# adaLN weight pieces moved from SP's DMA queue to GpSimd's, one burst per projection unit from a single buffer

## The chip, the cores and the metric

The kernel runs on one core of a Trainium2 chip. Its time is the device time of one execution in microseconds (us), from the runs listed below; a further execution was recorded by the hardware profiler, and every duration below is from that trace. The engines have these names: PE is TensorE (PEld its weight loads), DVE is VectorE, ACT is ScalarE, POOL is GpSimd, SP is SyncE, which here only issues DMAs. SPq and POOLq are the issuing sides of SP and GpSimd.

## What is computed

One layer of a conditioned decoder, for a prompt of 256 tokens and for 8 sample sequences of 8 tokens (320 rows in all, width 2048), with weights shared by both. All arrays are float32.

```python
mod = silu(c) @ w_ada + b_ada                    # (9, 6*2048): one row per sequence
sh1, sc1, g1, sh2, sc2, g2 = split(mod, 6)
h = rmsnorm(x, norm1_g) * (1 + sc1) + sh1
q, k, v, og, u, ga, gb, alr = split(h @ w_in)
o, s_new = gla(q, k, v, log_sigmoid(alr @ w_a2 + b_a) / 16, state_gla)
y_a = rmsnorm(o, gla_norm_g) * silu(og)
y_b = pool(u) * pool_scale
x = x + g1 * ((sigmoid(ga) * y_a + sigmoid(gb) * y_b) @ w_o)
h2 = rmsnorm(x, norm2_g) * (1 + sc2) + sh2
gate, up = split(h2 @ w_gu, 2)
y = rmsnorm(x + g2 * ((silu(gate) * up) @ w_down), final_norm_g)
```

The "adaLN" part is the first line: w_ada has 6 sections of 2048 columns, 100 MB in all, multiplied by only nine rows. Sections 0 and 1 (sh1, sc1) are needed before the first projection, section 2 (g1) after w_o, sections 3 and 4 (sh2, sc2) before the FFN, and section 5 (g2) after w_down.

## The kernel before

**Projections.** Each weight matrix streams from HBM once. `raw_chunk` (L131) loads a piece of 4 k-tiles by 256 columns, 512 KB, through SP's queue into one of three raw buffers. `split` (L141) makes a high half (ACT, L146) and the low remainder (DVE, L147), in four buffers each of two k-tiles. `mm3` (L159 to L162) adds three matmuls per k-tile and 128 columns. A unit (`proj`, L164) is 256 columns by 16 k-tiles: 4 pieces, 2 MB, 96 matmuls. PE works through the units in order; SP issues a piece when the DVE has freed its raw buffer.

**Stages.** The head of the program normalizes x, computes sections 0 and 1 and projects head 0 of four; then come the other three heads, eleven units each (L902 to L922: q, k, two of v, u, two each of og, ga and gb). While a head's units run, the GLA and pooling steps of the head before are taken from a queue (`pump`, ten steps after each unit) and run between them. Then come w_o (eight units, L964), the second norm, and the FFN in two parts: w_gu, then w_down (L1010 on).

**adaLN bursts.** Sections 4, 2, 3 and 5 are made in "bursts" (L239, L240): 24 bursts of 256 columns by 16 k-tiles (2 MB, sections 4, 2, 3), then two of 512 columns by 16 k-tiles (4 MB) and four of 512 columns by 8 k-tiles (2 MB) for section 5. `ada_load` (L256) takes a buffer of 16 KB per partition (for the 4 MB bursts 32 KB), with the tag "big", and lists its pieces of 1 MB; `ada_piece` (L247) issues one of them on SP, after the last weight piece; `ada_burst` (L263) does its matmuls (L279, the activations stationary, w_ada moving), transposes the result back (L292) and adds it up (L294). In heads 1 to 3 there is a burst after each of the units 3 to 10, with two buffers and one burst ahead. Burst 25 and 26 are loaded during w_o, in pieces that `x1_and_ada` (L955) issues between weight pieces, and done after the second norm's sum (L987). The last four are loaded and done in the first part of the FFN.

**GLA states.** Per head the old states of 8 sequences are 4 MB. `s_load` (L731) loads half of the sequences, 2 MB as two DMAs (d = 0, 1) on GpSimd, into a buffer of the same tag "big" as the bursts. `s_inter` (L740) multiplies by them on PE (L747), `s_state` (L763) updates them on DVE (L770) and GpSimd stores them back (L772). A tile framework decides the order on each engine when the program is built, and puts in the waits for buffers and data.

Of the kernel before, what the change touches and what calls it, by code (L numbers as in the profile page):

```python
# [1 line left out]

# [1 line left out]

# [7 lines left out]
F32 = mybir.dt.float32  # L12
# [67 lines left out]
def body(tc, A):  # L80
# [13 lines left out]
    def nm(s):  # L94
        uid[0] += 1
        return "%s_%d" % (s, uid[0])
# [30 lines left out]

    more = []
    last_raw = []

    def raw_chunk(src, nk, nn, pool=None, tag="raw", bufs=3):  # L131

# [26 lines left out]
    def mm3(ps, whi, wlo, xhi, xlo, start, stop):  # L159
        PE.matmul(ps, lhsT=whi, rhs=xhi, start=start, stop=False)  # L160
        PE.matmul(ps, lhsT=whi, rhs=xlo, start=False, stop=False)  # L161
        PE.matmul(ps, lhsT=wlo, rhs=xhi, start=False, stop=stop)  # L162

    def proj(w, col, k0, k1, xh, xl, between=None):  # L164

# [78 lines left out]
    ada_want = []  # L244
    ada_ps = []

    def ada_piece():  # L247

        n, t, r = ada_want.pop(0)
        sec, b, nb, k0, nk = BURSTS[n]  # L250
        step = min(nk, 16 // nb)
        col = (sec * KT + b) * P
        with tc.issue_after(last_raw[0]):
            nc.sync.dma_start(t[:, r:r + step], wada[:, k0 + r:k0 + r + step, col:col + nb * P])

    def ada_load(n, bufs):  # L256

# [2 lines left out]
            t = ada_raw[n] = apool[0].tile([P, nk, nb * P], F32, tag="big", bufs=bufs, name=nm("araw"))  # L260
            ada_want.extend((n, t, r) for r in range(0, nk, min(nk, 16 // nb)))

    def ada_burst(ahead, bufs):  # L263

        n = len(ada_done)
        sec, b, nb, k0, nk = BURSTS[n]
        ada_done.append(n)
        ada_load(n, bufs)
        while ada_want and ada_want[0][0] <= n:
            ada_piece()  # L270
        w = nb * P
        if k0 == 0:
            ada_ps[:] = [misc()]
        ps = ada_ps[0]
        first = True
        with tc.high_priority():
            for r in range(nk - 4, -1, -4):
                for j in range(4):
                    PE.matmul(ps[32 * j:32 * j + 32, 0:w], lhsT=scT[:, k0 + r + j, :], rhs=ada_raw[n][:, r + j, :],  # L279
                              start=k0 == 0 and first, stop=k0 + nk == KT and r == 0, tile_position=(0, 32 * j))  # L280
                first = False
        for m in range(n + 1, n + 1 + ahead):
            ada_load(m, bufs)
# [26 lines left out]
    def s3(ap):  # L310
        return ap.rearrange("p (b t) -> p b t", t=LS)
# [229 lines left out]
    def gla_steps(g):  # L541
# [188 lines left out]

        def s_load(gg):  # L731
            def f():
                t = apool[0].tile([P, 2, 4, DV], F32, tag="big", bufs=2, name=nm("S0"))
                for d in range(2):
                    nc.gpsimd.dma_start(t[:, d], A["state_gla"][0, 4 * gg:4 * gg + 4, h, d * P:(d + 1) * P, :]
                                        .rearrange("b p e -> p b e"))
                    E["S0", gg, d] = t[:, d]
            return f

        def s_inter(gg):  # L740
# [158 lines left out]
                gates(g0, kind, i, getattr(g0, kind)[:, 2 * i:2 * i + 2, :])  # L899
    queue += pst + st[:PSY] + [sig0] + psy + st[PSY:] + [merge_step(g0, E)]  # L900
    RATE = 10
    for h in range(1, H):  # L902
        pump(RATE)
        g = new_group(h)
        for ui, (kind, i, col) in enumerate(units(h)):
            if kind == "og" and i == 0:
                pump(len(queue))
                new_gates(g)
            ps = proj(win, col, 0, KT, hh, hl)
            evac(ps, g, kind, i, None)  # L910
            if kind == "u":
                pump(len(queue))
                st, E = gla_steps(g)
                pst, psy = pool_steps(g)
                queue += pst + st
            if ui > 2:
                ada_burst(0 if ui == 10 else 1, 2)
                while ada_want:
                    ada_piece()
            pump(RATE)  # L920
        queue += psy + [merge_step(g, E)]
    pump(len(queue))  # L922
# [29 lines left out]

    xs = fp.tile([P, KT, TS], F32, name="xs")
    tiny = fp.tile([P, 1], F32, name="tiny")
    def x1_and_ada(c):  # L955

        if c == 0:
            with tc.issue_after(last_raw[0]):
                for k in (2 * ui, 2 * ui + 1):
                    nc.sync.dma_start(x1[k], xspill[k])  # L960
        elif c < 12 and ada_want:
            ada_piece()

    for ui in range(8):  # L964
        if ui == 0:
            ada_load(AMIX, 2)
            ada_load(AMIX + 1, 2)
        ps = proj(wo, 256 * ui, 0, KT, mh, ml, between=x1_and_ada)
        for i in range(2):
            residual(ps, i, 2 * ui + i, 2)  # L970
            k = 2 * ui + i
            sq_acc(acc, k, k == 0)
            G.tensor_tensor(s3(xs[:, k]), s3(x1[k][:, TP:T]), mods(4, k), op=ALU.mult)
        if ui == 6:
            S.activation(tiny, epst, AF.Sqrt)

# [7 lines left out]

    more[:] = [fa, None]
    rs = rstd_bcast(acc)
    ada_burst(0, 2)  # L987
    ada_burst(0, 2)
# [21 lines left out]
    for pi, (f0, f1) in enumerate(parts):  # L1010
        ah, al = {}, {}
        for f in range(f0, f1, 2):
            sg = fa.tile([P, 2, T], F32, tag="sg", name=nm("sg"))
            if f == 0:
                pg, pu = projs(((wgu, f * P), (wgu, FF + f * P)), 0, KT, h2h, h2l)
                S.activation(sg, pg[:, :, 0:T], AF.Silu)
            else:
                pg = proj(wgu, f * P, 0, KT, h2h, h2l)
                S.activation(sg, pg[:, :, 0:T], AF.Silu)
                pu = proj(wgu, FF + f * P, 0, KT, h2h, h2l)  # L1020
            V.tensor_tensor(sg, pu[:, :, 0:T], sg, op=ALU.mult)
            th = f2.tile([P, 2, T], F32R, tag="ah%d" % ((f - f0) // 2), name=nm("ah"))
            tl = f2.tile([P, 2, T], F32R, tag="al%d" % ((f - f0) // 2), name=nm("al"))
            hilo(th, tl, sg)
            for j in range(2):
                ah[f + j], al[f + j] = th[:, j], tl[:, j]
            if pi == 0 and f >= 2:
                if f == 2:
                    ada_load(AEND, 1)
                if f in (4, 8, 12, 16):  # L1030
                    ada_burst(1, 1)
                if ada_want:
                    ada_piece()
        if pi == 0:
            bcx.close()
        else:
            hcx.close()
            yp = ctx.enter_context(tc.tile_pool(name="yp", bufs=1, side="right"))
            yn = [yp.tile([P, D], F32, name="yn%d" % i) for i in range(3)]
            xgs = [yp.tile([P, 3 * P], F32, name="xg%d" % i) for i in range(2)]  # L1040
            for xg in xgs:
                G.memset(xg[:, T:3 * P], 0.0)
        for ui in range(8):
            ps = proj(wdn, 256 * ui, f0, f1, ah, al)
            for i in range(2):
# [12 lines left out]
            if pi == 1 and ui == 5:  # L1058
                S.activation(tiny, acc2[:, 0:1], AF.Sqrt)
# [44 lines left out]
```

## Time and profile before

| | |
|---|---|
| runs | 2012.51, 2013.57, 2014.87 us; median 2013.57 |
| the profiled execution | 2015.12 us, its span 2013.2 us |
| mean granted clock of PE | 0.991 |
| moved by DMA | 400.60 MB, mean 199 GB/s |
| weight pieces (w_in), issue to landing | 4.7 us median, 512 KB |
| adaLN pieces, issue to landing | 11.0 us median, 1 MB |
| GLA state loads, issue to landing | 8.7 us median, 1 MB |

The page is read like this. Its first part gives the busy time of each engine. The second cuts the span into 40 slices of some 50 us; a digit is the busy share in tenths, PEclk the clock that PE was granted, DMA the busy share of the 16 DMA engines. Further views give busy times by stretch, who waited for whom, the chain of waits that ended last, the instructions in order of time, and the DMA queues: q1 is the hardware queue that SP feeds, q0 the software queue that GpSimd feeds. A DMA row "on SPq" is the time in which the queue took the request, not the transfer. The head lies at 0 to 225 us, heads 1 to 3 at about 225 to 890, w_o to 1040, the FFN to 2000.

### The profile page before, as it was taken

How to read it: one execution, taken by the hardware profiler on the slowest of the kernel's cores; microseconds unless marked ns; L12 is line 12 of the kernel's file. 1: busy time of each engine (PE TensorE's matmuls, PEld its weight loads, DVE VectorE, ACT ScalarE, POOL GpSimd, SP SyncE). 2: the span in 40 equal slices, each digit the busy share in tenths (PEclk: the TensorE clock that was granted, in tenths of full speed). 3: DMA queues.
4: the chain of work that ended last, by engine and by line, in shares of the span. 5: the costliest groups of instructions: out<-in, count | busy, mean ns of one | idle time of the engine just before them, and what ended most of it. 6: DMA issues, size and time to landing. Idle time of an engine off the chain costs nothing.

```text
span 2013.2 us, 34658 instructions
## 1 busy us (share of the span) xinstructions
PE 1946.5 (97%) x13808; PEld 1824.4 (91%) x13808; DVE 1000.4 (50%) x1918; ACT 828.1 (41%) x1484; POOL 121.1 (6%) x228
## 2 busy tenths in 40 slices
PE   5999999999999999998999999999999999999997
PEld 3779998888998898987979999999999999999997
DVE  2655655555355535663565444444444444444554
ACT  3323634643344333552445333333333343344443
POOL 1002100210011001100021000000000000000000
PEclk9999999999999999999999999999999999999998
DMA  9996457559765987489735655444444444444443
GB/s 320 346 333 232 128 178 249 184 189 333 234 216 191 294 248 240 150 281 340 243 117 166 203 166 188 160 152 150 142 157 152 147 149 155 148 147 147 147 141 100
DMA packets 350236, 400.60 MB, mean 199 GB/s; under 512 B 12417, under 2 KB 322209, under 8 KB 349737
## 3 DMA queue, kind: packets, MB, share of 16 engines
q1 hardware_dynamic: 338122, 358.29, 56.8%
q0 software_dynamic: 11952, 40.10, 5.5%
q8 instruction: 108, 1.77, 0.4%
q14 instruction: 54, 0.44, 0.1%
HBM read 373.90 MB, written 24.67 MB: 198 GB/s over the span
## 4 chain that ended last, share of the span: by engine, by line
PE 83%; DMA 9%; DVE 3%; issue 2%; ACT 1%; SPq 1%; POOL 0%; ACTq 0%; DVEq 0%
PE ps L160 25%; PE ps L162 25%; PE ps L161 25%; DMA raw<-w_in 3%; DMA raw<-w_o 2%; PE pm L279 2%; PE pm L220 1%; DMA S<-state_gla 1%; PE pm L125 1%; DVE wlo L147 1%; DVE S L770 1%; DMA o_gs<-S 1%; PE pm L747 1%; DMA vr<-b_ada 1%; DMA araw<-w_ada 1%
## 5 line engine op out<-in xcount | busy, mean ns | idle before, releaser
L147 DVE TENSOR_TENSOR wlo<-raw,whi 128x512 fp32r<-128x512 f32 x952 | 655.3, 694 | 798.5 <-ACT whi L146 795.1
L146 ACT CAST whi<-raw 128x512 fp32r<-128x512 f32 x952 | 585.2, 622 | 917.4 <-PE ps L161 775.7
L160 PE MATMUL ps<-hh,whi 128*128 128x320 f32 x1408 | 444.2, 316 | 10.1 <-ACT whi L146 9.8
L162 PE MATMUL ps<-hh,wlo 128*128 128x320 f32 x1408 | 438.3, 313 | 1.9 <-DVE wlo L147 1.8
L161 PE MATMUL ps<-hl,whi 128*128 128x320 f32 x1408 | 439.6, 312 | 0.0
L160 PE MATMUL ps<-h2h,whi 128*128 128x320 f32 x1408 | 435.8, 310 | 0.0
L161 PE MATMUL ps<-h2l,whi 128*128 128x320 f32 x1408 | 435.6, 309 | 0.0
L162 PE MATMUL ps<-h2h,wlo 128*128 128x320 f32 x1408 | 435.3, 309 | 0.0
L160 PEld LDWEIGHTS ps<-hh,whi 128*128 128x128 f32 x1408 | 265.5, 189 | 34.2 <-ACT whi L146 14.3
L162 PEld LDWEIGHTS ps<-hh,wlo 128*128 128x128 f32 x1408 | 264.8, 189 | 13.8 <-DVE wlo L147 6.1
L161 PEld LDWEIGHTS ps<-hl,whi 128*128 128x128 f32 x1408 | 265.7, 189 | 7.6 <-issue 6.4
L161 PEld LDWEIGHTS ps<-h2l,whi 128*128 128x128 f32 x1408 | 264.3, 188 | 3.4 <-issue 3.4
L160 PEld LDWEIGHTS ps<-h2h,whi 128*128 128x128 f32 x1408 | 264.3, 188 | 0.8 <-ACT h2h L997 0.8
L162 PEld LDWEIGHTS ps<-h2h,wlo 128*128 128x128 f32 x1408 | 264.3, 188 | 0.0
L160 PE MATMUL ps<-ah,whi 128*128 128x320 f32 x704 | 217.7, 309 | 0.0
L161 PE MATMUL ps<-al,whi 128*128 128x320 f32 x704 | 216.5, 308 | 0.0
L162 PE MATMUL ps<-ah,wlo 128*128 128x320 f32 x704 | 216.5, 308 | 0.0
L161 PEld LDWEIGHTS ps<-al,whi 128*128 128x128 f32 x704 | 132.0, 187 | 0.0
L160 PEld LDWEIGHTS ps<-ah,whi 128*128 128x128 f32 x704 | 131.9, 187 | 0.0
L162 PEld LDWEIGHTS ps<-ah,wlo 128*128 128x128 f32 x704 | 131.9, 187 | 0.0
L160 PE MATMUL ps<-mh,whi 128*128 128x320 f32 x256 | 80.3, 314 | 9.7 <-ACT whi L146 9.7
L162 PE MATMUL ps<-mh,wlo 128*128 128x320 f32 x256 | 80.1, 313 | 0.2 <-DVE wlo L147 0.2
(279 smaller groups left out, 1532.8 us busy)
## 6 DMA issues: line engine op xcount, KB each, us to landing
raw<-w_gu SPq DMA_DIRECT2D x176, 512.0 KB, 3.6
raw<-w_in SPq DMA_DIRECT2D x173, 512.0 KB, 4.7
araw<-w_ada SPq DMA_DIRECT2D x64, 1024.0 KB, 11.0
raw<-w_down SPq DMA_DIRECT2D x80, 512.0 KB, 3.5
raw<-w_ada SPq DMA_DIRECT2D x64, 512.0 KB, 6.7
S<-state_gla POOLq DMA_DIRECT2D x16, 1024.0 KB, 8.7
o_gs<-S POOLq DMA_DIRECT2D x16, 1024.0 KB, 6.2
raw<-w_o SPq DMA_DIRECT2D x32, 512.0 KB, 5.9
```

The source lines that it names most:

```text
L125: PE.transpose(out, in_, ident[:k, :k])
L146: S.copy(hi, raw)
L147: V.tensor_sub(lo, raw, hi.bitcast(F32))
L160: PE.matmul(ps, lhsT=whi, rhs=xhi, start=start, stop=False)
L161: PE.matmul(ps, lhsT=whi, rhs=xlo, start=False, stop=False)
L162: PE.matmul(ps, lhsT=wlo, rhs=xhi, start=False, stop=stop)
L220: PE.matmul(ps[32 * j:32 * j + 32, 0:w], lhsT=scT[:, k0 + i, :], rhs=raw[:, i, :], start=r == 0, stop=r == 3, tile_position=(0, 32 * j))
L279: PE.matmul(ps[32 * j:32 * j + 32, 0:w], lhsT=scT[:, k0 + r + j, :], rhs=ada_raw[n][:, r + j, :], start=k0 == 0 and first, stop=k0 + nk == ...
L747: PE.matmul(pt[32 * j:32 * j + 32, :], lhsT=qeP[:, d, 4 * gg + j, :], rhs=E["S0", gg, d][:, j], start=False, stop=d == 0, tile_position=(0 ...
L770: V.scalar_tensor_tensor(t[:, j], t[:, j], E["dec"][:, d, c:c + 1], pt, op0=ALU.mult, op1=ALU.add)
```

## The change

1. `ada_piece` issues on GpSimd in place of SP, and without the order after the last weight piece.
2. In heads 1 to 3 the bursts follow units 0, 1, 2, 3 and 7, 8, 9, 10 in place of 3 to 10. There is one buffer in place of two; the pieces of the next burst are asked for right after a burst, both at once. The first is asked for before head 1. A burst's matmuls are ordered after the last projection matmul issued.
3. GLA states get a tag of their own, "S0", with two buffers of 8 KB per partition: one for each d of a half group, in place of one 16 KB buffer for both.
4. The eight pieces of the two 4 MB bursts are issued on GpSimd, each after the GpSimd multiplication for one row block (`gi`), so two at the end of each of the first four w_o units, in place of two between the weight pieces of each of these units.
5. In the FFN a burst's two pieces are asked for together.

```diff
-    def ada_piece():
+    def ada_piece(after=None):
...
-        with tc.issue_after(last_raw[0]):
-            nc.sync.dma_start(t[:, r:r + step], wada[:, k0 + r:k0 + r + step, col:col + nb * P])
+        with tc.issue_after(after) if after is not None else nullcontext():
+            nc.gpsimd.dma_start(t[:, r:r + step], wada[:, k0 + r:k0 + r + step, col:col + nb * P])
...
+    def ada_all():
+        while ada_want:
+            ada_piece()
...
-        with tc.high_priority():
+        with tc.high_priority(), tc.issue_after(last_mm[0]):
...
-                t = apool[0].tile([P, 2, 4, DV], F32, tag="big", bufs=2, name=nm("S0"))
                 for d in range(2):
-                    nc.gpsimd.dma_start(t[:, d], A["state_gla"][0, 4 * gg:4 * gg + 4, h, d * P:(d + 1) * P, :]
+                    t = E["S0", gg, d] = lp.tile([P, 4, DV], F32, tag="S0", bufs=2, name=nm("S0"))
+                    nc.gpsimd.dma_start(t, A["state_gla"][0, 4 * gg:4 * gg + 4, h, d * P:(d + 1) * P, :]
...
+    BURST_UNITS = (0, 1, 2, 3, 7, 8, 9, 10)
+    ada_load(0, 1)
+    ada_all()
...
-            if ui > 2:
-                ada_burst(0 if ui == 10 else 1, 2)
-                while ada_want:
-                    ada_piece()
+            if ui in BURST_UNITS:
+                ada_burst()
+                if len(ada_done) < AMIX:
+                    ada_load(len(ada_done), 1)
+                    ada_all()
...
-        elif c < 12 and ada_want:
-            ada_piece()
...
-            G.tensor_tensor(s3(xs[:, k]), s3(x1[k][:, TP:T]), mods(4, k), op=ALU.mult)
+            gi = G.tensor_tensor(s3(xs[:, k]), s3(x1[k][:, TP:T]), mods(4, k), op=ALU.mult).ins
+            if ada_want:
+                ada_piece(gi)
...
-                if f == 2:
-                    ada_load(AEND, 1)
                 if f in (4, 8, 12, 16):
-                    ada_burst(1, 1)
-                if ada_want:
-                    ada_piece()
+                    ada_burst()
+                if f in (2, 4, 8, 12):
+                    ada_load(len(ada_done), 1)
+                    ada_all()
```

What this does to the order on the engines is shown at two places. In the rows, `raw` is a weight piece, `araw` a buffer of a burst, `S` a state buffer; the numbers count buffers and differ between the two programs; "x2" is two pieces of 1 MB.

The first place is the last units of head 1, some 450 to 500 us into the program. SP's queue before:

```order
L138 DMA raw_5176<-w_pool 128x2x512
L254 DMA araw_4339<-w_ada 128x8x256 x2
L254 DMA araw_4505<-w_ada 128x8x256 x2
L138 DMA raw_5227<-w_in 128x4x256
L138 DMA raw_5261<-w_in 128x4x256
L138 DMA raw_5295<-w_in 128x4x256
L254 DMA araw_4671<-w_ada 128x8x256 x2
L254 DMA araw_4837<-w_ada 128x8x256 x2
L138 DMA raw_5329<-w_in 128x4x256
```

GpSimd's queue there now:

```order
L771 DMA o_gs<-S_667_3917 128x4x512
L771 DMA o_gs<-S_668_3919 128x4x512
L735 DMA S_1023_6077<-state_gla 128x4x512
L255 DMA araw_4681<-w_ada 128x8x256 x2
L735 DMA S_1024_6079<-state_gla 128x4x512
L255 DMA araw_4847<-w_ada 128x8x256 x2
L255 DMA araw_5011<-w_ada 128x8x256 x2
```

Before, two bursts, 4 MB, stood in a row ahead of the next three weight pieces, twice. Now SP's queue holds weight pieces alone, and the bursts stand behind each other in GpSimd's queue, among the state stores and loads, each waiting for PE to be done with the one before. On PE seven of the 24 bursts now come 76 projection matmuls after the burst before, nine come 81 to 94 after it, and the rest more than that.

The second place is w_o. SP's queue before:

```order
L254 DMA araw_9326<-w_ada 128x8x256 x2
L138 DMA raw_9869<-w_o 128x4x256
L138 DMA raw_9904<-w_o 128x4x256
L138 DMA raw_9955<-w_o 128x4x256
L960 DMA x_4_9625<-xspill 128x320
L960 DMA x_5_9626<-xspill 128x320
L138 DMA raw_9991<-w_o 128x4x256
L254 DMA araw_9640<-w_ada 128x4x512 x4
L254 DMA araw_9641<-w_ada 128x4x512
L138 DMA raw_10026<-w_o 128x4x256
```

GpSimd's queue there now:

```order
L255 DMA araw_9340<-w_ada 128x8x256 x2
L973 TENSOR_TENSOR xs<-x_0_9629,mod 128x64
L255 DMA araw_9648<-w_ada 128x4x512
L973 TENSOR_TENSOR xs<-x_1_9630,mod 128x64
L255 DMA araw_9648<-w_ada 128x4x512
L973 TENSOR_TENSOR xs<-x_2_9631,mod 128x64
L255 DMA araw_9648<-w_ada 128x4x512
```

Before, five pieces stood in a row ahead of one w_o piece. Now each follows one multiplication on GpSimd, which in turn waits for the end of a w_o unit.

More of the change, by code (lines that the diff above doesn't have):

```diff
@@ L1 @@
-from contextlib import ExitStack
+from contextlib import ExitStack, nullcontext
 import numpy as np
@@ L129, in body @@
     last_raw = []
+    last_mm = []
     def raw_chunk(src, nk, nn, pool=None, tag="raw", bufs=3):
@@ L161, in mm3 @@
         PE.matmul(ps, lhsT=whi, rhs=xlo, start=False, stop=False)
-        PE.matmul(ps, lhsT=wlo, rhs=xhi, start=False, stop=stop)
+        last_mm[:] = [PE.matmul(ps, lhsT=wlo, rhs=xhi, start=False, stop=stop).ins]
     def proj(w, col, k0, k1, xh, xl, between=None):
@@ L261, in ada_load, with ada_burst @@
             ada_want.extend((n, t, r) for r in range(0, nk, min(nk, 16 // nb)))
-    def ada_burst(ahead, bufs):
+    def ada_all():
+        while ada_want:
+            ada_piece()
+    def ada_burst():
         n = len(ada_done)
@@ L267, in ada_burst @@
         ada_done.append(n)
-        ada_load(n, bufs)
-        while ada_want and ada_want[0][0] <= n:
-            ada_piece()
         w = nb * P
@@ L281, in ada_burst @@
                 first = False
-        for m in range(n + 1, n + 1 + ahead):
-            ada_load(m, bufs)
         if k0 + nk < KT:
@@ L732, in f @@
             def f():
-                t = apool[0].tile([P, 2, 4, DV], F32, tag="big", bufs=2, name=nm("S0"))
                 for d in range(2):
-                    nc.gpsimd.dma_start(t[:, d], A["state_gla"][0, 4 * gg:4 * gg + 4, h, d * P:(d + 1) * P, :]
+                    t = E["S0", gg, d] = lp.tile([P, 4, DV], F32, tag="S0", bufs=2, name=nm("S0"))
+                    nc.gpsimd.dma_start(t, A["state_gla"][0, 4 * gg:4 * gg + 4, h, d * P:(d + 1) * P, :]
                                         .rearrange("b p e -> p b e"))
-                    E["S0", gg, d] = t[:, d]
             return f
@@ L954, in body, with x1_rows @@
     tiny = fp.tile([P, 1], F32, name="tiny")
-    def x1_and_ada(c):
+    def x1_rows(c):
         if c == 0:
@@ L960, in x1_and_ada @@
                     nc.sync.dma_start(x1[k], xspill[k])
-        elif c < 12 and ada_want:
-            ada_piece()
+    ada_load(AMIX, 2)
+    ada_load(AMIX + 1, 2)
     for ui in range(8):
[L965 to L968, printed above, removed]
+        ps = proj(wo, 256 * ui, 0, KT, mh, ml, between=x1_rows)
         for i in range(2):
@@ L986, in body @@
     rs = rstd_bcast(acc)
-    ada_burst(0, 2)
-    ada_burst(0, 2)
+    ada_burst()
+    ada_burst()
     h2h = [hp.tile([P, T], F32R, tag="hh%d" % k, name="h2h%d" % k) for k in range(KT)]
@@ L1027, in body @@
             if pi == 0 and f >= 2:
-                if f == 2:
-                    ada_load(AEND, 1)
                 if f in (4, 8, 12, 16):
-                    ada_burst(1, 1)
-                if ada_want:
-                    ada_piece()
+                    ada_burst()
+                if f in (2, 4, 8, 12):
+                    ada_load(len(ada_done), 1)
+                    ada_all()
         if pi == 0:
```

## The prediction

> **What bounds the kernel now.** I read the page first, for which engine is full and where it is not.
>
> ```profile
> PE 1946.5 (97%) x13808; PEld 1824.4 (91%) x13808; DVE 1000.4 (50%) x1918; ACT 828.1 (41%) x1484; POOL 121.1 (6%) x228
> ...
> PE   5999999999999999998999999999999999999997
> ...
> PEclk9999999999999999999999999999999999999998
> DMA  9996457559765987489735655444444444444443
> ```
>
> TensorE is the bound, with 97% of the span. The change removes no matmul and adds none, so all that it can give back is time in which TensorE waits or runs at a lower clock. The DMA digits say where to look: they reach 9 in the middle of the attention stage and around w_o, while the FFN sits at 4. The next view, busy time by stretch, cuts the span at those places (columns: PE, PEld, DVE, ACT, POOL busy, granted clock, DMA share, GB/s).
>
> ```profile
> core 0: us, PE busy (x) PEld busy (x) DVE busy (x) ACT busy (x) POOL busy (x), PEclk, DMA share, GB/s
> ...
> 175.00:350.00 175.00, 174.49 (x1206) 164.05 (x1204) 103.44 (x207) 81.83 (x156) 25.13 (x45) 1.00 0.62 196
> 350.00:375.00 25.00, 21.55 (x156) 18.73 (x155) 11.90 (x27) 7.71 (x14) 8.96 (x20) 1.00 0.82 261
> 375.00:550.00 175.00, 173.47 (x1311) 156.45 (x1313) 85.35 (x166) 77.05 (x140) 11.84 (x15) 1.00 0.74 235
> 550.00:575.00 25.00, 21.91 (x155) 19.83 (x147) 11.22 (x25) 8.79 (x19) 2.92 (x7) 0.93 0.91 295
> 575.00:760.00 185.00, 184.40 (x1395) 167.09 (x1397) 93.31 (x182) 80.37 (x147) 17.75 (x28) 1.00 0.74 230
> 760.00:785.00 25.00, 21.34 (x143) 19.74 (x136) 11.63 (x26) 8.59 (x19) 2.36 (x6) 0.93 0.87 282
> 785.00:890.00 105.00, 103.67 (x722) 93.63 (x721) 64.95 (x130) 56.09 (x105) 17.46 (x26) 1.00 0.59 185
> 890.00:930.00 40.00, 40.00 (x348) 35.48 (x346) 21.91 (x51) 17.16 (x33) 0.55 (x2) 1.00 1.09 349
> 930.00:962.00 32.00, 20.42 (x144) 18.65 (x143) 9.37 (x20) 7.02 (x14) 0.55 (x2) 0.85 0.98 334
> ...
> 1100.00:1950.00 850.00, 850.00 (x5815) 843.39 (x5815) 387.48 (x628) 334.32 (x552) 0.23 (x2) 1.00 0.50 156
> ```
>
> From 1100 to 1950 us TensorE never waits: 850 us for 5,815 matmuls, 0.146 us each. Between 175 and 962 us its idle time stands almost whole in four short stretches: 3.45 us at 350, 3.09 at 550, 3.66 at 760 and 11.58 at 930. Three of these have a lower clock as well. The waits of the stretch 175 to 1000 us name the causes, for TensorE and for ScalarE, which makes the high half of each weight:
>
> ```profile
> PE ps L160 <- ACT whi L146: 19.2, 9, 9.5
> PE pm L747 <- DMA S<-state_gla: 2.8, 3, 1.3
> PE pm L279 <- DMA araw<-w_ada: 2.2, 2, 1.7
> ...
> ACT whi L146 <- DMA raw<-w_in: 62.2, 20, 6.4
> ACT whi L146 <- DMA raw<-w_o: 31.0, 8, 13.1
> ```
>
> So TensorE waits for ScalarE, and ScalarE for the weights' own DMA. SP's own queue at w_o, and under it the chain of waits there, show why that DMA is late:
>
> ```profile
> 936.50 7.60 SPq L254 DMA_DIRECT2D araw<-w_ada  x5
> 944.20 2.87 SPq L138 DMA_DIRECT2D raw<-w_o  x1
> ```
>
> ```profile
> 944.20 13.60 DMA raw<-w_o
> 957.89 0.63 ACT whi L146
> ...
> 959.20 0.27 PE ps L161
> ...
> 961.79 0.27 PE ps L161
> ```
>
> Five adaLN pieces of 1 MB went into SP's queue ahead of one w_o piece; that piece landed 13.60 us after its issue, and TensorE came back at half pace (0.27 us a matmul instead of 0.146) and was still there 3.5 us later. The DMA view of 885 to 933 us shows the jam that preceded it:
>
> ```profile
> DMA packets 16420, 16.81 MB, mean 350 GB/s; under 512 B 397, under 2 KB 16213, under 8 KB 16416
> ...
> araw<-w_ada SPq DMA_DIRECT2D x8, 1024.0 KB, 11.0
> ```
>
> 48 us at 350 GB/s, nothing spare. At 550 us the same thing happens with the GLA states: two state loads from GpSimd and two adaLN pieces from SP start within 1.3 us of each other (quoted below), and the weights queued behind the pieces come last.
>
> **What the change does to those waits.** Pieces no longer stand in SP's queue. What decides the weights' fate is then how the DMA engines divide between GpSimd's queue and SP's. The DMA view of 557 to 560 us, where states (q0) and SP's traffic (q1) are both waiting, shows it:
>
> ```profile
> DMA packets 461, 1.13 MB, mean 377 GB/s; under 512 B 2, under 2 KB 246, under 8 KB 461
> ...
> q0 software_dynamic: 217, 0.88, 77.3%
> q1 hardware_dynamic: 244, 0.25, 24.9%
> ```
>
> About one packet each in turn (217 against 244), but GpSimd's packet holds 4 KB and SP's 1 KB. So GpSimd's stream moves at 0.88 MB / 3 us = 293 GB/s and SP keeps 83 GB/s. The weights need a 0.52 MB piece per 24 matmuls, 3.5 us, which is 150 GB/s. A 2.1 MB burst takes 7.2 us at 293 GB/s, and meanwhile the weights fall behind by 7.2 x 67 = 0.48 MB, one piece. Three raw buffers and two pieces' worth of split buffers stand against that. Before, the same 2.1 MB in the same queue stopped the weights altogether for 6 us, and SP often held two bursts in a row (12 us), which is what the buffers could not cover.
>
> The gains, by stretch, with what I expect to stay:
>
> - 930 to 962: 11.58 us idle, and 3.5 us at half pace, 1.75 us: 13.3. The eight large pieces now go out two per w_o unit, about every 14 us. I take 12.
> - 550 to 575: 3.09 idle plus 7% of 25 us of clock, 1.75: 4.8. The state loads now have buffers of their own and start when the old state has left, not beside a double burst. I take 4.5.
> - 760 to 785: 3.66 plus 1.75 is 5.4; the same cause. I take 5.
> - 350 to 375: 3.45 us, no loss of clock; two bursts in a row in SP's queue. Four bursts now go into the first four units of head 1, in a stretch with 196 GB/s on average. I take 3.
> - The waits for states at L747, 2.8 us: the second half group is now fetched per half, each half as soon as its own store has landed, not after both. I take 2.
> - Idle time left in the other stretches (0.51, 1.53, 0.60 and 1.33 us; part of it the state waits just counted): 1.5.
>
> Together 28 us.
>
> What it adds. **A burst with one buffer**: its 2.1 MB may be asked for only when the previous burst is off TensorE, and GpSimd's queue waits for that too. No row has such a load, so I bound it by the nearest, two state loads of 1 MB, also from GpSimd. Two rows of the timeline at 551 us, then the times to landing of the state loads issued at 552 and at 352 us, and from the chain of waits the length of a burst:
>
> ```profile
> 551.91 1.50 POOL L735 DMA_DIRECT2D S<-state_gla  x2 [92.18 <-PE pm L125]
> 553.21 5.11 SPq L254 DMA_DIRECT2D araw<-w_ada  x2
> ```
>
> ```profile
> DMA to landing us min/median/max: 5.9/7.4/9.0
> ...
> DMA to landing us min/median/max: 8.4/10.0/11.5
> ```
>
> ```profile
> 669.54 1.86 PE pm L279 x32
> ```
>
> The pair issued at 551.91 was whole 9.0 us after its second issue, 9.8 after the first. The pair at 352 us took 11.5 and 12.3. In the new order seven of the 24 bursts stand only 76 projection matmuls after the one before, 11.1 us at 0.146; the others have 81 or more. So a burst is between 1.3 us early and 1.2 us late at those seven: 0 to 8 us in all. I take 2, since the weights' stream is all that most of them meet, as at 551.91. Cover gone, each microsecond of landing costs one at each of the seven. **GpSimd's queue**: behind a waiting piece stand state loads and stores, the copies for the pooling buffer and the w_a2 load. In the order of the changed kernel these serve steps that come 40 or more projection matmuls after the burst that releases the piece, 5.8 us, and a state load's issue is 0.75 us of GpSimd's time; nothing added. **Three pile-ups**: at the end of a head's GLA the queue holds two state stores, a state load, a burst and another load, six times 1.05 MB. That is 21 us at 293 GB/s, with the weights at 83: 1.8 MB, 3.4 pieces, while TensorE in 21 us less a 1.86 us burst and some 2 us of state matmuls wants 4.9. Short by 1.5 pieces, which full buffers cover and half-full ones do not: 0 to about 5 us each, and 1.7 of clock. I take 1.5 in all. In the FFN two pieces at a time, where TensorE has no wait and DMA is half idle: nothing. Issues taken off SP: nothing, because SP mostly waits for a free buffer, by the list of its waits:
>
> ```profile
> SPq L138 <- DVE wlo L147: 1212.4, 398, 11.4
> ```
>
> One rule of the Trainium skill speaks against moving the requests. In the page "DMA: Bandwidth & Descriptors", section "SWDGE vs HWDGE vs iDMA", GpSimd writes its descriptors into SBUF, and VectorE in its two-port mode can lock it out there, which SP's requests never meet. The trace does not bear it out:
>
> ```profile
> L735 POOL DMA_DIRECT2D S<-state_gla x16: 748/753/765, 180.2 to 854.0; - x16
> ```
>
> All sixteen issues lie within 17 ns of each other with VectorE half busy. By the rule, two issues per burst held up by a VectorE operation each would make the seven close bursts late and the sum a few microseconds worse; by the row, nothing.
>
> Sum: 28 - 2 - 1.5 = 24.5 us. The profiled execution took 2015.12 us (span 2013.2), 1.55 us above the median of the runs shown, 2013.57. So 2015.1 - 24.5 = 1990.6 in its terms, and about 1989 for a median.
>
> **The rivals.**
>
> - *The weights starve at the pile-ups* (chance 0.20). For it: 83 GB/s against 150 needed. Against: outside a pile-up the weights may have the whole 350 GB/s and win back a piece in 0.52 / (0.350 - 0.150) = 2.6 us, so the buffers should be full when it begins. Three places at 5 + 1.75 us, less the 1.5 already in, give 1989 + 18.8 = 2008; at 3.5 + 1.75 us, buffers a third full, 2003, which I write.
> - *Slower: the single buffer decides* (0.08). If the pieces, whose rows are 1 KB and not the states' 2 KB, get no more than half of 350 GB/s, a burst takes 2.1 / 0.175 = 12 us plus some 2 us of issue and landing, 14. The point is 11.1 us. Then seven bursts are 2.9 us late and the nine at 81 to 94 matmuls (11.8 to 13.7 us) 1.3 on average, 32 us together; a wait of 3 us brought the 1.75 us of clock above, 12 more for seven. 1989 + 44 - 2 = 2031. The weights' own waits would be gone, but TensorE would stand at L281 instead.
> - *No change* (0.07). The bytes stay, the 48 us at 350 GB/s stay, and what the weights don't wait for in SP's queue they wait for on the DMA engines: 28 us given back and taken again, 2010 to 2015. Against it: 550 to 575 averages 295 GB/s and 350 to 375 only 261, so order, not bytes, made those waits. The Trainium skill, same page, section "Issuing engines are not separate DMA queues", would have it so: requests from several engines run on the same DMA engines, and only issue time is saved. The packets above bear out the shared engines; that nothing else is saved, no run here shows yet.
>
> **How the numbers follow.** The group of one projection line, whose mean, 309 ns, is used here:
>
> ```profile
> L161 PE MATMUL ps<-h2l,whi 128*128 128x320 f32 x1408 | 435.6, 309 | 0.0
> ```
>
> The forecast, 1989, has 0.65. Its own low end is all 28 us and nothing added, 1985.6, and some more, because a matmul's row lasts 0.309 us at a pace of 0.146, so that waits shorter than the difference don't show as idle time; I go to 1976. Its high end is 8 + 15 us of added cost instead of 3.5, about 2009, which takes in the first rival. Outside lie the second and third, 0.15, and a little of the first. What a measurement of this kernel can tell from no change is about 0.2%, 4 us. Faster: 0.65 + 0.20 = 0.85; same 0.07; slower 0.08.
>
> **What would show it.** Right: no idle stretch over 2 us on TensorE between 175 and 1000 us, no clock below 1.00 there, the wait of ScalarE for w_o near zero; in the DMA view the pieces under GpSimd with 8 to 11 us to landing, and q0 at 4 KB a packet. Wrong: waits at L281 for araw (second rival); waits of whi for w_in just after state loads (first); packets of 1 KB in q0; or a w_o wait of the old size.

## The result, and the profile after

The changed kernel took 1992.62 us (median of 4 runs, 1991.17 to 1995.78), the kernel before 2013.04 (4 runs, 2011.40 to 2014.87). The ratio is 0.990, with a 95% interval of 0.9883 to 0.9918: 20 us faster. The profiled execution took 1991.17 us (span 1989.4), the fastest of its four, against 2015.12 before, which is slower than all four runs of before: 24.0 us less, where the prediction's sum was 24.5 and the medians differ by 20.4.

The page of the changed kernel: busy times, and the two DMA queues (packets, MB, share of 16 engines).

```profile
PE 1938.0 (97%) x13808; PEld 1819.7 (91%) x13808; DVE 1002.8 (50%) x1918; ACT 829.4 (42%) x1483; POOL 179.3 (9%) x292
...
q1 hardware_dynamic: 279754, 291.17, 46.8%
q0 software_dynamic: 29360, 107.21, 15.6%
```

TensorE does the same 13,808 matmuls. GpSimd's queue q0 has gained 67.1 MB (40.10 before) in 17,408 more packets (11,952 before): 3.85 KB each. Busy time by stretch, with the columns of the prediction's table:

```profile
175.00:350.00 175.00, 173.37 (x1233) 160.26 (x1232) 95.78 (x194) 79.96 (x155) 32.08 (x53) 1.00 0.65 207
350.00:375.00 25.00, 22.46 (x168) 20.55 (x167) 18.98 (x41) 9.36 (x16) 9.32 (x19) 0.99 0.98 321
375.00:550.00 175.00, 173.85 (x1300) 156.99 (x1299) 89.40 (x170) 78.03 (x143) 26.70 (x34) 0.99 0.74 240
550.00:575.00 25.00, 25.00 (x192) 23.86 (x191) 11.66 (x24) 9.67 (x20) 4.79 (x9) 1.00 0.89 289
575.00:760.00 185.00, 183.67 (x1370) 167.89 (x1373) 96.84 (x192) 83.20 (x153) 29.92 (x42) 1.00 0.73 234
760.00:785.00 25.00, 25.00 (x207) 23.18 (x198) 12.92 (x26) 8.66 (x15) 6.31 (x12) 1.00 0.88 283
785.00:890.00 105.00, 105.00 (x746) 94.94 (x749) 66.77 (x137) 57.87 (x109) 17.34 (x25) 1.00 0.61 195
890.00:930.00 40.00, 39.10 (x316) 36.04 (x305) 20.29 (x44) 16.96 (x31) 6.01 (x8) 1.00 0.97 325
930.00:962.00 32.00, 31.58 (x212) 30.83 (x211) 17.76 (x41) 13.40 (x26) 7.41 (x11) 1.00 0.91 303
```

At 550 and 760 us TensorE no longer waits, and its clock is whole. At 930 us 0.42 us of idle time is left of 11.58 (with 0.90 at 890 us, where there was none), at 350 us 2.54 against 3.45. From 175 to 962 us the idle time was 25.75 us and is 7.97: 17.8 us of the 23.8 by which the span is shorter. Of the rest some 3.5 us is clock, as an estimate: three stretches of 1.75 us of loss before, by the prediction's working, against one of 1.7 now (last section). No view here assigns the last 2.5 us. The bytes still flow at the same rate (289 GB/s in place of 295 at 550 us): what changed is who waits for them. The waits from 175 to 1000 us, of TensorE and then of ScalarE:

```profile
PE ps L161 <- ACT whi L147: 3.5, 4, 2.4
PE pm L281 <- DMA araw<-w_ada: 1.5, 3, 1.0
```

```profile
ACT whi L147 <- DMA raw<-w_in: 45.9, 19, 7.7
ACT whi L147 <- DMA raw<-w_o: 28.6, 8, 6.3
```

TensorE's wait for the weights' high half fell from 19.2 us to 3.5, and no wait for states is left in the list (2.8 before). ScalarE's waits for w_o are still 28.6 us of 31.0, but the longest is 6.3 us in place of 13.1, and TensorE's own longest wait for the high half is 2.4 us in place of 9.5: the buffers between the two engines cover most of such a wait.

One stall of over 2 us is left between 175 and 1000 us, at 370 us. The chain of waits there, and the DMA queues from 350 to 372 us:

```profile
359.20 12.94 DMA raw<-w_in
...
372.24 0.63 ACT whi L147
...
373.63 0.41 PE ps L163
```

```profile
q0 software_dynamic: 1405, 5.37, 72.5%
q1 hardware_dynamic: 2016, 2.01, 29.1%
```

A w_in piece took 12.94 us to land while GpSimd's queue moved a state store, two state loads and a burst, 5.37 MB in 22 us or 244 GB/s, and left the weights 91. That is the prediction's first rival, the pile-up, at one of its three places; the late request below tests it.

### The profile page after: what moved, and what is told of

Same layout as the page of the kernel before. It is cut to its first block, busy times and chain, and to the rows that moved or that the text cites. A ratio compares the mean times of both kernels' runs of the same rounds, so it can differ in the third digit from the quotient of the medians.

```text
span 1989.4 us, 34665 instructions
## 1 busy us (share of the span) xinstructions
PE 1938.0 (97%) x13808; PEld 1819.7 (91%) x13808; DVE 1002.8 (50%) x1918; ACT 829.4 (42%) x1483; POOL 179.3 (9%) x292
## 3 DMA queue, kind: packets, MB, share of 16 engines
q1 hardware_dynamic: 279754, 291.17, 46.8%
q0 software_dynamic: 29360, 107.21, 15.6%
## 4 chain that ended last, share of the span: by engine, by line
PE 90%; DMA 6%; DVE 2%; ACT 1%; issue 0%; SPq 0%; POOL 0%; ACTq 0%; DVEq 0%
PE ps L161 26%; PE ps L163 26%; PE ps L162 26%; PE pm L281 3%; DMA araw<-w_ada 2%; DMA raw<-w_in 2%; PE pm L125 2%; PE pm L221 1%; DMA raw<-w_o 1%; PE pm L767 1%; PE pm L746 1%; PE pm L715 1%; DMA vr<-b_ada 1%; DVE wlo L148 1%; ACT whi L147 0%
## 5 line engine op out<-in xcount | busy, mean ns | idle before, releaser
L255 POOL DMA_DIRECT2D araw<-w_ada x64 | 54.9, 862 | 448.5 <-PE pm L281 419.2
```

What stands on the lines that cost most here:

```text
L255: nc.gpsimd.dma_start(t[:, r:r + step], wada[:, k0 + r:k0 + r + step, col:col + nb * P])
```

## The experiments

All times are medians beside runs of the kernel before on the same chip. The ratio is to those; the changed kernel's is 0.990 [0.9883, 0.9918]. The runs of before differ by up to 3 us from set to set, so kernels are best compared by their ratios.

| kernel | us | before beside it | ratio [95%] |
|---|---|---|---|
| queue alone | 2011.62 | 2012.85 | 0.9995 [0.9985, 1.0005] |
| w_o alone | 2003.49 | 2012.85 | 0.9951 [0.9937, 0.9966] |
| queue and spread w_o | 2006.45 | 2015.80 | 0.9955 [0.9939, 0.9971] |
| spaced on SP | 2013.32 | 2012.85 | 1.0005 [0.9992, 1.0019] |
| changed, pieces on SP | 2000.76 | 2013.17 | 0.9934 [0.9917, 0.9950] |
| changed, w_o at once | 2010.57 | 2013.17 | 0.9986 [0.9977, 0.9995] |
| changed, states in pairs | 1998.79 | 2015.80 | 0.9915 [0.9897, 0.9932] |
| changed, units 3 to 10 | 1995.80 | 2013.17 | 0.9910 [0.9895, 0.9925] |
| changed, late request, 1st try | 1991.34 | 2012.85 | 0.9895 [0.9879, 0.9911] |
| changed, late request, 2nd try | 2000.65 | 2013.17 | 0.9937 [0.9922, 0.9951] |
| changed, w_o pieces later | 1991.83 | 2015.80 | 0.9883 [0.9867, 0.9898] |
| units 3 to 10 and w_o later | 1987.03 | 2015.80 | 0.9860 [0.9841, 0.9878] |

**The queue alone** (edit of the kernel before):

```diff
-            nc.sync.dma_start(t[:, r:r + step], wada[...])
+            nc.gpsimd.dma_start(t[:, r:r + step], wada[...])
```

> The kernel before, with one word changed: the adaLN pieces are issued on GpSimd, with the old units, two buffers, shared state buffers, and w_o's pieces unspaced. My theory (pieces must not stand in the weights' queue): the weights' queue is free, so the short stretches in heads 1 to 3 go, about 10 of the 20 us; at w_o all eight pieces run at once in GpSimd's queue, 28 us in which the weights are short by (150 - 83) x 28 = 1.9 MB, so that half of the 11 us there stays. About 1998 us. Rival (the order and spacing of the bursts is what counts, not the queue): no gain, 2010 to 2015. Rival (states in buffers of their own count): states now stand behind pieces in one queue and wait, so no gain or a loss, 2013 or more.

No gain, as the rival of order and spacing had it; my 1998 us fell. Its page has the very queues of the changed kernel (q0 29360 packets, 107.21 MB), so the same bytes went the same way, and the time did not move. By stretch, two of the old stalls are gone and a new one stands between them:

```profile
550.00:575.00 25.00, 25.00 (x174) 24.99 (x173) 15.79 (x32) 9.70 (x19) 2.65 (x9) 1.00 0.50 152
575.00:760.00 185.00, 179.58 (x1352) 161.32 (x1351) 89.26 (x175) 79.22 (x146) 31.90 (x43) 0.98 0.74 242
760.00:785.00 25.00, 25.00 (x174) 24.98 (x173) 14.99 (x30) 9.88 (x19) 0.91 (x5) 1.00 0.58 184
```

GpSimd's timeline before the new stall, and the chain in it:

```profile
665.55 0.76 POOL L772 DMA_DIRECT2D o_gs<-S  x1 [3.69 <-DVE S L770]
668.51 0.90 POOL L254 DMA_DIRECT2D araw<-w_ada  x1 [2.20 <-PE pm L279]
669.67 0.89 POOL L254 DMA_DIRECT2D araw<-w_ada  x1 [0.26 <-issue]
673.19 1.76 POOL L254 DMA_DIRECT2D araw<-w_ada  x2 [2.63 <-DMA o_gs<-S]
```

```profile
672.31 13.38 DMA raw<-w_in
...
689.00 0.63 PE psy L160
```

With two buffers, two bursts go out within 6.5 us beside a state store, and a w_in piece needs 13.38 us. The weights no longer stand behind the bursts, but they starve beside them, here and again at 884 us, where a w_o piece took 13.57 us: the pile-up, with a pair of bursts beside the states.

**w_o alone** (the kernel before, with the eight large pieces as changed):

```diff
-            nc.sync.dma_start(...)
+            (nc.sync if after is None else nc.gpsimd).dma_start(...)
...
+            gi = G.tensor_tensor(s3(xs[:, k]), ...).ins
+            if ada_want:
+                ada_piece(gi)
```

> The kernel before, with the eight large pieces of w_o alone put on GpSimd, each after the multiplication for one row block; heads 1 to 3 as before. My theory: the w_o stretch is repaired and nothing else, 11 us, 2002 us. By the prediction's own sizes 12, 2001. Rival (all gain comes from the heads, and the w_o stretch jams with 48 us at 350 GB/s whatever the order): 2013.

About 10 us (0.49% of 2013), as expected: half of the whole gain. Its stretches show w_o repaired and the heads' stall at 550 us as before:

```profile
550.00:575.00 25.00, 21.66 (x151) 20.30 (x144) 11.67 (x26) 8.98 (x19) 2.92 (x7) 0.87 0.88 291
...
930.00:962.00 32.00, 30.29 (x222) 28.95 (x223) 17.25 (x37) 12.91 (x24) 5.66 (x10) 1.00 0.95 325
```

**w_o's pieces all at once** (the changed kernel without the spreading):

```diff
     ada_load(AMIX + 1, 2)
+    ada_all()
...
-            if ada_want:
-                ada_piece(gi)
```

> The changed kernel with the eight large pieces asked for at once at the start of w_o, still on GpSimd. Theory (the weights starve beside a long burst: 83 GB/s against 150 for 28 us, short by 1.9 MB, 3.6 pieces of 3.5 us, less some two pieces of buffers): 5 to 9 us more, 1997 to 2002 us. In the run with the queue alone changed, a w_o piece took 19.7 us to land there, and TensorE stood 6.9 us. Rival (the queue is enough, spreading adds nothing): 1992 to 1994 us.

Far worse than both the theory and its rival: 0.86% of 2013, 17 us, is lost again. The chain at 902 us, and the queues from 905 to 925 us:

```profile
901.98 14.29 DMA x<-xspill
...
916.89 24.70 DMA raw<-w_o
```

```profile
q0 software_dynamic: 1549, 5.96, 78.6%
q1 hardware_dynamic: 1580, 1.65, 25.0%
```

One packet each in turn, 298 GB/s for GpSimd's queue and 82.5 for SP's, where the prediction had worked out 293 and 83 from three microseconds of before. I had taken off two pieces for buffers that were full; but the rows of x1, 2.6 MB in all, wait in the same starved queue (14.29 us), and a w_o piece then took 24.70. So at w_o the queue without the spreading loses.

**Spacing alone, on SP** (the kernel before, heads 1 to 3):

```diff
+            ps = proj(win, ..., between=lambda c: c in (0, 8) and ada_want and ada_piece())
...
-                while ada_want:
-                    ada_piece()
```

> The kernel before, with the pieces of heads 1 to 3 still in SP's queue and two buffers, but one piece at a time between the weight pieces (after the first and after the third of a unit) in place of bursts of two and four in a row; w_o as before. My theory (the queue counts): a piece in SP's queue may still be stuck behind a buffer that isn't free and holds the weights up; a part of the heads' 10 us comes back, 2008 to 2013. Rival (spacing counts): 1 MB at 350 GB/s is 3 us, less than a weight piece lasts (3.5 us), so the buffers cover it and the heads' 10 us come back whole, 2003 us.

No gain, neither a part nor the whole. The waits of TensorE from 175 to 1000 us changed their name:

```profile
PE pm L279 <- DMA araw<-w_ada: 14.2, 9, 4.1
PE ps L160 <- ACT whi L146: 7.5, 3, 6.8
```

Late pieces made the bursts late in place of the weights. So neither the queue alone nor the spacing alone gives anything in the heads.

**The changed kernel with its pieces on SP:**

```diff
-        with tc.issue_after(after) if after is not None else nullcontext():
-            nc.gpsimd.dma_start(t[:, r:r + step], ...)
+        with tc.issue_after(last_raw[0]):
+            nc.sync.dma_start(t[:, r:r + step], ...)
```

> The changed kernel with the queue alone put back: the pieces go into SP's queue behind the last weight piece, with the new units, one buffer, states in buffers of their own, and the large pieces spread over w_o. Theory (a queue of its own is needed, given this schedule): SP waits at each piece until the burst before is off TensorE, with weights behind it, and then for 2.1 MB, 6 us at 350 GB/s; the buffers hold some 7 us of weights. Half of the gain or more is lost, 2003 to 2030 us, with waits of whi for w_in in heads 1 to 3. Rival (the schedule and the states' buffers made the gain, and the queue is only a place to put the requests): 1991 to 1996 us.

7 to 8 us slower than the changed kernel (by ratios and by medians; the intervals touch at 0.9917 and 0.9918), and still 0.66%, 13 us, faster than before: between the theory's range and the rival's, and in neither. SP's waits from 175 to 1000 us, and its timeline at the stall of 370 us:

```profile
SPq L255 <- PE pm L281: 37.9, 18, 8.2
```

```profile
352.62 6.39 SPq L255 DMA_DIRECT2D araw<-w_ada  x2
359.40 16.94 SPq L139 DMA_DIRECT2D raw<-w_in  x4
```

SP stands 37.9 us for the single buffer, with weights behind it. A second place is w_o, where the pieces are spread here too:

```profile
890.00:930.00 40.00, 36.37 (x299) 32.09 (x298) 20.83 (x47) 16.27 (x29) 0.55 (x2) 0.99 0.97 321
930.00:962.00 32.00, 30.20 (x196) 29.93 (x196) 16.17 (x34) 12.11 (x22) 3.33 (x4) 0.96 0.94 326
```

TensorE is idle for 5.43 us of these two stretches, against 1.32 in the changed kernel and 11.58 before. So the new schedule and buffers give about two thirds of the gain with the pieces still on SP, and the queue adds 7 to 8 us to that; without them it adds nothing. The Trainium skill's "DMA: Bandwidth & Descriptors", "Issuing engines are not separate DMA queues", says that a second issuing engine saves only the time of issuing. The run with the queue alone agrees (0.9995). This one does not fit it: a request that waits for a buffer holds up what is queued behind it, and moving the request moves that.

**States in one buffer for both halves** (the changed kernel):

```diff
-                    t = E["S0", gg, d] = lp.tile([P, 4, DV], F32, tag="S0", bufs=2, ...)
+                t = lp.tile([P, 2, 4, DV], F32, tag="S0", bufs=1, ...)   # E["S0", gg, d] = t[:, d]
```

> The changed kernel with the GLA states in one 16 KB buffer for both d of a half group, in place of two of 8 KB: a load then waits for the stores of both. Memory and all else as changed. Theory (the states' own, smaller buffers let each half be fetched as soon as its own store has landed, the prediction's 2 us at the state matmuls): 1 to 4 us more, 1993 to 1997 us, with waits of TensorE for S of 2 us or more. Rival (the splitting is idle, states are in time either way): 1991 to 1994 us and no such wait.

By its ratio, some 1996 us, it falls into the theory's range. But the interval overlaps the changed kernel's, so a loss is not settled by the times, and TensorE's wait for S that I expected is 0.2 us. The profiled execution, 2002.59 us, is the slowest of its four. It has a stall elsewhere, in GpSimd's timeline and the chain at 683 us:

```profile
678.79 0.90 POOL L255 DMA_DIRECT2D araw<-w_ada  x1 [1.46 <-PE pm L281]
...
684.03 1.51 POOL L736 DMA_DIRECT2D S<-state_gla  x2 [3.22 <-DMA o_gs<-S]
```

```profile
682.60 12.93 DMA raw<-w_in
```

Two state loads start together beside a burst, and the weights wait. In the changed kernel they start one at a time.

**Units 3 to 10 again** (the changed kernel):

```diff
-    BURST_UNITS = (0, 1, 2, 3, 7, 8, 9, 10)
+    BURST_UNITS = (3, 4, 5, 6, 7, 8, 9, 10)
```

> The changed kernel with the bursts after the units 3 to 10 again, as before the change; queue, single buffer, states' buffers and w_o as changed. Theory of the prediction (the queue does it, a single buffer is seldom late): 1992 to 1996 us. Rival (the units were what kept 4 MB from standing in a row while the states move: with them the heads' 10 us go): 1999 to 2004 us.

The times don't tell it from the changed kernel, as the prediction's theory had it. The stretch at 350 us is better (23.93 us busy), w_o worse, with this in its chain:

```profile
912.17 14.42 DMA raw<-w_o
```

Two more of the bursts fall into w_o, and their pieces meet the large ones.

**A later request, twice.** The first try only moved the request in the text; it was meant to follow unit 6.

```diff
-                if len(ada_done) < AMIX:
+            if ui in (0, 1, 2, 6, 7, 8, 9, 10) and len(ada_done) < AMIX:
```

> The changed kernel, but the burst after unit 7 is asked for after unit 6 and not already after unit 3, so that its 2.1 MB are not in GpSimd's queue with the state stores and loads. In the trace of the changed kernel a w_in piece took 12.9 us to land at 359 to 372 us while GpSimd's queue moved 5.4 MB in 22 us, and TensorE stood 2.5 us and ran at half pace for some 3.4 us, 1.7 us of loss. Theory (the weights starve at a pile-up, the prediction's first rival, come true at one place of three): that stall goes, 1.5 to 4 us, 1989 to 1991 us, and the piece lands in less than 8 us. Rival (the stall is VectorE's, which was late with the weights' low half because of the merge steps at 355 to 359 us): the stall stays, 1992.6.

It is the changed kernel over again, since the request still went out once the burst before had ended:

```profile
351.52 1.76 POOL L255 DMA_DIRECT2D araw<-w_ada  x2 [1.90 <-PE pm L281]
```

In the second try the request has an order after the last store of the pooling step:

```diff
+            pool_out[:] = [nc.gpsimd.dma_start(A["o_pp"][...], ...).ins]
...
+                    ada_piece(pool_out[0] if ui == 6 else None)
```

> What the run before under nearly the same name meant to do and did not: its request still went out at 351.5 us, since nothing held it there. Here the burst after unit 7 is asked for behind the last store of the pooling step, at about 376 us, in each of the heads 1 to 3. Theory (pile-up: weights starve beside 5.4 MB of GpSimd's traffic): the stall at 370 us goes, 2 to 4 us, 1988.5 to 1990.5 us; w_in pieces land in less than 9 us there. Rival (the states alone, 4 MB in and out at that place, or VectorE's lateness, make the stall): it stays, 1991 to 1993 us.

Its stretches at 350 and 930 us, and its chain at 911 us:

```profile
350.00:375.00 25.00, 25.00 (x190) 23.60 (x190) 20.61 (x46) 11.05 (x18) 9.32 (x21) 1.00 0.86 269
...
930.00:962.00 32.00, 28.59 (x197) 26.42 (x196) 14.14 (x32) 9.70 (x19) 4.80 (x8) 0.95 0.79 266
```

```profile
911.23 20.87 DMA raw<-w_o
```

The stall at 370 us is gone with the burst, and the w_in pieces there land in 5.5 us in place of 8.6: the states alone don't make it, and VectorE, no less busy than in the changed kernel (20.61 us, 18.98 there), doesn't either. But the time is 7 to 8 us worse, outside both ranges. Some of that is in head 2, where TensorE is idle for 3.7 us between 470 and 490 us; most is at w_o. One more burst was then left for w_o, four pieces went out from 912 to 917 us, and a w_o piece took 20.87 us.

**w_o's pieces later**, with the changed units and with units 3 to 10:

```diff
-            if ada_want:
+            if ada_want and k >= 6:
                 ada_piece(gi)
```

> The changed kernel with the eight large pieces of w_o put off by three units: two each at the end of units 3 to 6 in place of 0 to 3. Theory (all loss at w_o comes of pieces of two bursts that stand in GpSimd's queue together; in the changed kernel four pieces go out at 907 to 917 us, and TensorE loses little there): 0 to 2 us less, 1990 to 1993 us. Rival (the large pieces now come late for the bursts after the second norm, at 1020 us): more than 1994 us, with a wait for araw there.

> The changed kernel with the bursts after units 3 to 10 again and the eight large pieces of w_o put off by three units. With the units alone the heads were faster and w_o slower: the stretch 350 to 375 us had TensorE busy for 23.93 us in place of 22.46, but w_o had stalls of 3.7 and 2.9 us at 923 and 959 us, where four and more pieces in GpSimd's queue held a w_o piece up for 14.4 us. Theory (it is the number of pieces standing together that decides, at w_o as in the heads): w_o's loss goes, the heads' gain stays, 1984 to 1990 us. Rival (the units 3 to 10 are worse in themselves): 1994 to 1998 us as before.

With the changed units the gain is not settled (0.9883 against 0.990, intervals overlapping). With units 3 to 10 it is: 0.9860, 28 us below before and, by the ratios, 8 below the changed kernel (5.6 by the medians), and the intervals don't touch. The stretches of this fastest kernel:

```profile
350.00:375.00 25.00, 23.85 (x180) 22.19 (x180) 13.17 (x28) 10.11 (x17) 9.07 (x20) 1.00 0.91 293
...
890.00:930.00 40.00, 37.83 (x314) 34.32 (x313) 17.55 (x38) 14.80 (x29) 6.46 (x10) 1.00 0.95 308
930.00:962.00 32.00, 32.00 (x239) 30.87 (x238) 16.98 (x36) 12.29 (x22) 2.93 (x6) 1.00 0.70 233
```

The large pieces now come after the last small burst, so no four pieces stand together, and neither the heads nor w_o have a clock below 1.00.

**Queue and spread, with the old buffers** (the kernel before with the first two edits of this section):

```diff
+            nc.gpsimd.dma_start(t[:, r:r + step], ...)
...
+            if ada_want:
+                ada_piece(gi)
```

> The kernel before with the pieces on GpSimd and the large pieces of w_o spread, two per unit; units 3 to 10, two buffers, and the buffers that bursts and states share, as before. Theory (with two buffers GpSimd's queue takes 4 MB in a row right beside the states, so that the weights starve in heads 1 to 3; only w_o is repaired): 1999 to 2004 us. Rival (queue and spreading are all of the change's gain, and single buffer and states' buffers add nothing): 1991 to 1996 us.

It stays with the gain of the run with only w_o changed, and by its ratio, 2004 us, at the upper end of the theory's range. The stall of the queue alone is there again, and w_o is repaired from 930 us on:

```profile
575.00:760.00 185.00, 179.04 (x1348) 160.71 (x1347) 88.77 (x174) 79.14 (x145) 31.25 (x42) 0.98 0.75 240
930.00:962.00 32.00, 30.64 (x222) 28.46 (x222) 13.55 (x31) 9.88 (x19) 5.04 (x9) 1.00 0.87 301
```

The units are not what is missing, since the changed kernel with units 3 to 10 keeps its gain. What is left is one burst at a time, states with a tag of their own, and the order of a burst's matmuls after the last projection matmul. Which of these it is stays open: two buffers for bursts beside two for states, 16 KB more per partition, were not tried, nor was that order alone.

## Why the prediction was right, and where it was not

- **Sign and size.** 24.5 us forecast, 24.0 in the profiled executions, 20.4 in the medians. That the sum came so close is in part luck: the two profiled executions lie at opposite ends of their runs, and inside the sum the stretch at 350 us gave nothing of its 3 us while the 2 us for the single buffer were not spent.
- **930 to 962, 12 us.** Right: 11.16 us of idle time gone, and the lower clock. The w_o edit alone gave about 10. The step named two causes, pieces off SP and spreading, and it takes both: on GpSimd and unspread they cost 17 us, and spread but on SP, with all other pieces there too, 5.43 us of idle time stay between 890 and 962.
- **550 and 760, 4.5 and 5 us.** Right in size: 3.09 and 3.66 us of idle time are gone and the clock with them. The cause given was the states' own buffers. The run with the queue alone clears these two stretches as well, with the old buffers, but has 5.42 us of idle time between them instead; so what had to be gained was that no stall takes their place, and which part of the new buffers and order does that stays open.
- **350 to 375, 3 us.** Wrong: the idle time fell by 0.9 us, to 2.54 from 3.45, and 1.7 us of clock was lost that was not lost before, so the place gave nothing. The step that failed is the price of the three pile-ups, 1.5 us in all. One alone cost 2.5 us of idle time and 1.7 of clock (last section). The rival had asked for buffers that are not full when it begins. What the late request showed is that the burst among the states decides.
- **The state matmuls, 2 us.** Right in size, and by luck: no wait for S is left in the list, but none is left either in the run with the queue alone, with the old buffers, and with one buffer for both halves it is 0.2 us. So the reason given, that each half is fetched on its own, is not shown.
- **One buffer, 2 us of cost.** The wait at L281 is 1.5 us (2.2 before), so its price was nothing. The prediction missed what it may be for: with one buffer no two bursts run side by side among the states. Counted as a cost, it is one of the conditions of which, by the run with the old buffers, at least one is needed for the queue to gain anything in the heads.
- **The signs.** "No idle stretch over 2 us, no clock below 1.00" failed once, at 370 us; 8 to 11 us to landing and 4 KB a packet held (8.5 us and 3.85 KB). "The wait of ScalarE for w_o near zero" was wrong as a sign: 28.6 us of it stayed and cost almost nothing. The longest wait (13.1, now 6.3) would have been the sign.
- **No change, 0.07.** It held for the queue alone, and was wrong for the whole. What I wrote against it, order and not bytes, is what the runs show; but I had expected the queue by itself to bring that order.
- **Slower by the single buffer, 0.08.** Pieces landed in 8.5 us, below the point of 11.1, and waits at L281 are 1.5 us: excluded.

## What to carry to other kernels

Moving a stream of large loads to another issuing queue did not by itself relieve the stream it shared a queue with; it turned a wait in line into a share of the bandwidth, and the share went by packet size. Limit how much of the background stream can be outstanding at once and keep it away from other background transfers, which together with the states' own buffers gave 13 of the 20 us here; a queue of its own then gave the rest. Look at the longest wait ahead of the bound engine rather than at the sum: 28.6 us of ScalarE's waits for w_o, none over 6.3 us, cost TensorE almost nothing.

## What the hardware showed unexpectedly

TensorE's clock fell after a wait that had already ended. In the changed kernel TensorE was idle for 2.54 us of the stretch 350 to 375 us, all of it between 370 and 374 us; the stretches that follow, with the granted clock third from the right:

```profile
374.00:376.00 2.00, 2.00 (x12) 2.00 (x11) 1.47 (x3) 1.48 (x3) 0.99 (x3) 0.65 0.42 78
376.00:378.00 2.00, 2.00 (x9) 2.00 (x9) 0.69 (x1) 0.28 (x1) 0.95 (x3) 0.50 0.97 270
378.00:380.00 2.00, 2.00 (x15) 1.97 (x14) 0.69 (x1) 0.62 (x1) 0.00 (x0) 1.00 0.69 233
```

The loss is 0.35 x 2 + 0.50 x 2 = 1.7 us on top of the wait, the price that the prediction had taken for such stalls.

In the run with w_o's pieces all at once both queues were full from 905 to 925 us, and the DMA engines took 1549 packets of q0 and 1580 of q1: 5.96 MB against 1.65. The Trainium skill's page "DMA: Bandwidth & Descriptors", "Queues, rings and completion order", has the engines take turns by packets, and this agrees. The prediction had taken its 4 KB packets from the states, whose rows are 2 KB, and its second rival asked whether pieces with rows of 1 KB would do worse. They did not: the 64 pieces of w_ada, most of them with rows of 1 KB, went in 17,408 packets of 3.85 KB from GpSimd, and before the change in 58,368 of 1.15 KB from SP (q1: 338,122 packets, now 279,754). So the issuing engine, and not the load, set the size of the packets, and with it the share: 3.6 to 1 with both queues full.
